# Weight loads of 512 KB through six buffers in place of 1 MB through three

## The chip, the cores and the metric

The kernel runs on one core of a Trainium2 chip. The metric is device time in microseconds (us) of one execution. The engines are TensorE (PE; PEld is its weight load), VectorE (DVE), ScalarE (ACT), GpSimd (POOL) and SyncE (SP). SP's queue issues the weight transfers.

## The reference

Two blocks of two layers each work on 256 rows of width 1024 in float32. A layer of the first block has a mixer (a linear recurrence, attention with a forget gate, retention), cross attention to a memory, and a gated feed-forward stage. A layer of the second block has a feed-forward stage, a second mixer (mixer2: sparse attention with compressed keys and values, two further attention branches, three gates), and another feed-forward stage. Cut to what loads weights:

```python
def swiglu(h, w_gate, w_up, w_down):
    return (jax.nn.silu(h @ w_gate) * (h @ w_up)) @ w_down
...
    def compress(t, w1, w2):
        blocks = t[:, cmp_idx] + cmp_pos[:, None, :]
        blocks = blocks.transpose(0, 3, 1, 2, 4).reshape(B, G, n_cmp, CMP_LEN * Dh)
        return jax.nn.silu(blocks @ w1) @ w2
```

## The kernel before

All weights are read once from HBM, some 366 MB, in the order in which they are used. Class `Weights` plans, loads and prepares them. `plan` cuts a matrix into *chunks*, one transfer each (two where halves or a second matrix are put side by side), and a chunk into *pieces*, the unit that products are made from. A chunk is up to `CHUNK` = 2048 numbers wide in each of 128 partitions, 1 MB; a piece up to `PIECE` = 1024, 512 KB. So most chunks hold two pieces.

`_load` takes the next chunk into one of `NRAW` = 3 buffers (tile `raw`) by a transfer on SP's queue. `_split` makes a piece usable: ScalarE casts it to a rounded high part (`whi`), VectorE subtracts that from the original for the low part (`wlo`). With the activations in two parts as well (`thi`, `tlo`), each product of float32 numbers is three products on TensorE: `whi,thi`, `wlo,thi`, `whi,tlo`. There are `NPIECE` = 6 buffers for split pieces, so `_split` runs up to five pieces ahead of the products.

When a chunk's last piece has been split, its `raw` buffer is released and `_load` is called for the next chunk at once. The weights of the compression in mixer2 (`nsa_cmp_k_w1_2`, `nsa_cmp_v_w1_2`) are planned with `split=False`: TensorE reads them from `raw`, and their buffer is released only in `done`, behind the products on the chunk's last piece:

```python
                if last:
                    self.made += 1
                    del self.raw[ci]
                    self._load()
                    continue
```

The order of all instructions is fixed when the program is built. `Pace` keeps an estimate of each engine's time, and `pump` puts side work (attention steps, norms) between the products when that estimate says it is ready. SP's queue is in order: a load that waits for its buffer holds back what stands behind it, the small transfers too (constants, memory rows, `kvd`, `hk`, `btiles`). Transfers of SP and ScalarE take eight semaphores in turn (DMAHW0 to DMAHW7), and each waits until the transfer that had its semaphore before, eight places earlier, has landed.

In mixer2, `plan_mixer2` puts the four compression chunks between the chunks of `w_in_2`, one behind each of the first chunks of columns 1816 and up. `nat_blocks` makes the products (accumulators `acc`), and a callback takes two compression pieces at the places `CMP_AT` (tiles `o<-raw`). Other names of the trace: `aux` and `o` are PSUM banks of the attention steps, `nngm` row maxima, `rn` and `rs` scores of two branches, `t` gate values and copies, `bt` bias tiles, `hk` bias rows read back from DRAM, `mem` the memory rows of the cross attention.

The program records through a helper, so that all its instructions have line 153; places are told by tile names.

Of the kernel before, what the change touches and what calls it, by code (L numbers as in the profile page):

```python
# [20 lines left out]
EPS = 1e-6  # L21
NEG = -1e30
NPIECE = 6
NRAW = 3
PIECE = 1024
CHUNK = 2048

CMP_AT = (1, 3, 5, 7)
RET_HEADS = 4
# [128 lines left out]
class Weights:  # L158


    def __init__(self, nc, ctx, tc):
        self.nc = nc
        self.raw_pool = ctx.enter_context(nc.pool(tc, name="w_raw", bufs=NRAW))
        self.pool = ctx.enter_context(nc.pool(tc, name="w_split", bufs=NPIECE))
# [4 lines left out]
    def plan(self, ap, c0, c1, k0, k1, a_chunk, a_piece, split=True, gain=None, halves=0, beside=None):  # L169

        b = c1 - c0
        if halves:
            v = ap.rearrange("(g r d) n -> g d r n", g=2, r=halves)
        for k in range(k0, k1, a_chunk):
            a = min(a_chunk, k1 - k)
            ci = len(self.chunks)
            if halves:
                parts = [(slice(64 * g, 64 * g + 64), v[g][:, k : k + a, c0:c1]) for g in (0, 1)]
            else:
                parts = [(slice(0, P), ap[k * P : (k + a) * P, c0:c1].rearrange("(a p) n -> p a n", p=P))]  # L180
            parts = [(ps, slice(0, b), v_) for ps, v_ in parts]
            if beside is not None:
                parts.append((slice(0, P), slice(b, 2 * b), beside[k * P : (k + a) * P, c0:c1].rearrange("(a p) n -> p a n", p=P)))
            self.chunks.append((parts, a, b * (1 if beside is None else 2)))
            for j in range(0, a, a_piece):
                n = min(a_piece, a - j)
                self.pieces.append([ci, j, n, b * (1 if beside is None else 2), split, j + n >= a, None, list(range(k + j, k + j + n)), gain])
# [7 lines left out]
    def _load(self):  # L195
        if self.loaded >= len(self.chunks):
            return
        parts, a, b = self.chunks[self.loaded]
        t = self.raw_pool.tile([P, CHUNK], F32, tag="raw", name=f"raw{self.loaded}")
        v = t[:, : a * b].rearrange("p (a n) -> p a n", a=a)  # L200
# [74 lines left out]
def tile_two_blocks(ctx, tc, I, out):  # L275
# [1680 lines left out]
    nc.sync.dma_start(x[:, 1, :], I["x"][0, P:, :])  # L1956
    for _ in range(NRAW - 1):
        W._load()
# [129 lines left out]
```

## Time and profile before

| | |
|---|---|
| median of 3 runs | 2094.27 us (2092.91 to 2097.39) |
| profiled execution | 2093.85 us, span of the core 2092.1 us |
| TensorE, busy | 2038.4 us, 97% of the span |
| VectorE, busy | 1251.7 us, 60% |
| ScalarE, busy | 1098.7 us, 53% |
| transfers | 380.79 MB, mean 182 GB/s |
| SP's queue | 366.46 MB, 52.9% of the 16 DMA engines' span |
| loads of `raw` from `w_in` | 65 of 1024 KB, median 5.2 us from issue to landing |

A row of a timeline gives start and duration in us, the engine, the operation, the tiles it writes and reads, the shape and a count; in brackets stands how long the engine had been idle and who ended that. In the chain of waits a row is a piece of the chain that ended last. Matmuls are pipelined, so their durations overlap.

### The profile page before, as it was taken

Reading aid. Unit: us, or ns where it says so; the run is one execution under the profiler, and the core shown is the slowest. Engines: PE = TensorE matmul, PEld = TensorE weight load, DVE = VectorE, ACT = ScalarE, POOL = GpSimd, SP = SyncE. Lnnn points to the kernel's source line nnn. Section 1 sums busy time; section 2 is a strip of 40 time slices with the busy share of each in tenths; the row PEclk is TensorE's granted clock in tenths of the full one; section 3 lists DMA queues with packets and bytes.
Section 4 is the critical chain, followed back from the end, with each engine's and each line's share of the span. In section 5 each row is a group of like instructions: output and inputs, shape, how many; then the busy total and the mean of one; then the engine's idle time right before and its main releaser. Section 6 shows DMA issues by size and latency. Waiting matters only on the chain.

```text
span 2092.1 us, 27297 instructions
## 1 busy us (share of the span) xinstructions
PE 2038.4 (97%) x10446; PEld 1675.9 (80%) x10446; DVE 1251.7 (60%) x2123; ACT 1098.7 (53%) x1844; POOL 89.6 (4%) x112
## 2 busy tenths in 40 slices
PE   7999999999999999999999999999999998999999
PEld 6788888888787788788887678888888886778887
DVE  6666565556764755555464667664555565666553
ACT  5556465445564654555445555553554455456542
POOL 0210000001200000000010000000000010000000
PEclk9999999999999999999999999999999999999999
DMA  7555565645465555555555455555555465455552
GB/s 241 184 189 194 184 202 181 219 153 195 162 222 171 184 199 191 165 197 181 204 173 194 137 147 181 192 175 196 181 187 193 163 192 197 132 155 188 176 199 102
DMA packets 200610, 380.79 MB, mean 182 GB/s; under 512 B 14288, under 2 KB 70400, under 8 KB 200480
## 3 DMA queue, kind: packets, MB, share of 16 engines
q1 hardware_dynamic: 188960, 366.46, 52.9%
q10 hardware_dynamic: 11520, 12.59, 1.9%
q8 instruction: 82, 1.34, 0.2%
q14 instruction: 48, 0.39, 0.1%
HBM read 372.03 MB, written 6.99 MB: 181 GB/s over the span
## 4 chain that ended last, share of the span: by engine, by line
PE 81%; DVE 6%; ACT 5%; DMA 4%; issue 2%; POOL 0%; SPq 0%; ACTq 0%; DVEq 0%; POOLq 0%
PE acc L153 73%; PE aux L153 6%; DVE wlo L153 2%; DMA raw<-in_w_in_dram 2%; PE o L153 2%; ACT whi L153 2%; DMA hk<-ud 1%; ACT rn L153 1%; DMA nb<-cdram 0%; ACT thi L153 0%; DVE h L153 0%; DMA bt<-btiles 0%; ACT cpr L153 0%; DMA mem<-in_mem_dram 0%; DVE tlo L153 0%
## 5 line engine op out<-in xcount | busy, mean ns | idle before, releaser
L153 PE MATMUL acc<-whi,thi 128*128 128x512 f32 (+1 forms) x1760 | 702.1, 399 | 4.5 <-ACT kvout L153 2.7
L153 PE MATMUL acc<-wlo,thi 128*128 128x512 f32 (+1 forms) x1760 | 683.0, 388 | 3.5 <-DVE wlo L153 3.3
L153 PE MATMUL acc<-whi,tlo 128*128 128x512 f32 (+1 forms) x1760 | 683.8, 389 | 2.4 <-DVE tlo L153 2.3
L153 DVE TENSOR_TENSOR wlo<-raw,whi 128x1024 fp32r<-128x1024 f32 (+1 forms) x370 | 444.7, 1213 | 313.8 <-ACT whi L153 311.6
L153 ACT CAST whi<-raw 128x1024 fp32r<-128x1024 f32 (+1 forms) x370 | 378.5, 1038 | 252.9 <-PE acc L153 195.5
L153 DVE SCALAR_TENSOR_TENSOR wlo<-raw,prm,whi 128x512 fp32r<-128x512 f32 (+1 forms) x592 | 392.6, 719 | 177.2 <-ACT whi L153 176.9
L153 ACT ACTIVATE whi<-raw,prm 128x512 fp32r<-128x512 f32 (+1 forms) x592 | 372.2, 696 | 92.9 <-PE acc L153 89.4
L153 PEld LDWEIGHTS acc<-whi,thi 128*128 128x128 f32 x1760 | 332.8, 189 | 80.1 <-issue 12.3
L153 PEld LDWEIGHTS acc<-whi,tlo 128*128 128x128 f32 x1760 | 332.2, 189 | 73.2 <-DVE tlo L153 5.5
L153 PEld LDWEIGHTS acc<-wlo,thi 128*128 128x128 f32 x1760 | 333.0, 189 | 67.5 <-DVE wlo L153 6.5
L153 PE MATMUL acc<-whi,ahi 128*128 128x512 f32 x528 | 206.8, 392 | 0.3
L153 PE MATMUL acc<-whi,alo 128*128 128x512 f32 x528 | 205.6, 389 | 0.0
L153 PE MATMUL acc<-wlo,ahi 128*128 128x512 f32 x528 | 205.5, 389 | 0.0
L153 POOL TENSOR_TENSOR r<-v,mhalf 128x1 f32<-128x1 f32 (+3 forms) x46 | 49.5, 1076 | 1661.0 <-DVE v L153 1661.0
L153 DVE SCALAR_TENSOR_TENSOR silu<-acc,r,silu 128x512 f32<-128x512 f32 (+1 forms) x72 | 47.5, 702 | 118.1 <-PE acc L153 94.1
L153 PEld LDWEIGHTS acc<-whi,ahi 128*128 128x128 f32 x528 | 99.1, 188 | 21.6 <-ACT whi L153 1.5
L153 PEld LDWEIGHTS acc<-whi,alo 128*128 128x128 f32 x528 | 99.1, 188 | 20.5
L153 PEld LDWEIGHTS acc<-wlo,ahi 128*128 128x128 f32 x528 | 99.2, 188 | 20.2
L153 PE MATMUL acc<-thi,whi 128*128 128x256 f32 x384 | 113.4, 295 | 0.0
L153 ACT ACTIVATE silu<-acc,r 128x512 f32<-128x512 f32 (+1 forms) x72 | 43.1, 650 | 127.5 <-PE acc L153 127.5
L153 PE MATMUL acc<-tlo,whi 128*128 128x256 f32 x384 | 108.5, 283 | 0.0
L153 PE MATMUL acc<-thi,wlo 128*128 128x256 f32 x384 | 108.5, 282 | 0.0
(299 smaller groups left out, 1823.9 us busy)
## 6 DMA issues: line engine op xcount, KB each, us to landing
raw<-in_w_in_dram SPq DMA_DIRECT2D x65, 1024.0 KB, 5.2
raw<-in_ffn_w_down_dram SPq DMA_DIRECT2D x44, 1024.0 KB, 4.8
raw<-in_ffn_w_gate_dram SPq DMA_DIRECT2D x40, 1024.0 KB, 5.0
raw<-in_ffn_w_up_dram SPq DMA_DIRECT2D x40, 1024.0 KB, 5.0
raw<-in_w_down_dram SPq DMA_DIRECT2D x22, 1024.0 KB, 4.9
raw<-in_w_gate_dram SPq DMA_DIRECT2D x20, 1024.0 KB, 5.0
raw<-in_w_up_dram SPq DMA_DIRECT2D x20, 1024.0 KB, 4.9
raw<-in_w_out_dram SPq DMA_DIRECT2D x16, 1024.0 KB, 4.9
```

Of the source, the lines that this page charges most:

```text
L153: return f(*args, **kwargs)
```

## The change

A chunk becomes 1024 numbers wide in each partition, and there are six buffers in place of three. `plan` reduces every chunk to the pieces that fit, at least one: a chunk of 512 columns is now two of the 128-row blocks of its matrix instead of four, one piece. The compression chunks are halved in the same way.

```diff
-NRAW = 3
+NRAW = 6
 PIECE = 1024
-CHUNK = 2048
+CHUNK = 1024
...
     def plan(self, ap, c0, c1, k0, k1, a_chunk, a_piece, split=True, gain=None, halves=0, beside=None):
 
         b = c1 - c0
+
+        a_chunk = min(a_chunk, max(1, CHUNK // (b * (1 if beside is None else 2)) // a_piece) * a_piece)
         if halves:
```

A load is now put in the program behind the release that stands six releases before it, where it was three chunks before. The start loads six chunks ahead instead of three.

SP's queue in the first mixer2, before (`raw175` and `raw177` are compression weights for keys, `raw179` for values; a DVE wait is for the subtraction behind which the load's buffer is free, a PE wait for products on compression weights):

```order
L153 DMA raw176_9415<-in_w_in_2_dram 128x4x512 [waits DMAHW4_49,DVE_49]
L153 DMA raw177_9470<-in_nsa_cmp_k_w1_2_dram 128x8x256 [waits DMAHW1_49,DVE_49]
L153 DMA raw178_9622<-in_w_in_2_dram 128x8x256 [waits DMAHW4_49,DMAHW2_49,DVE_49]
L153 DMA raw179_9670<-in_nsa_cmp_v_w1_2_dram 128x8x256 [waits DMAHW3_49,PE_49]
L153 DMA raw180_9704<-in_w_in_2_dram 128x4x512 [waits DMAHW2_49,DVE_49]
```

The same place in the changed program:

```order
L153 DMA raw350_9788<-in_nsa_cmp_k_w1_2_dram 128x4x256 [waits DMAHW4_49,DVE_49]
L153 DMA raw351_9824<-in_nsa_cmp_k_w1_2_dram 128x4x256 [waits DMAHW5_49,DVE_49]
L153 DMA raw352_9950<-in_w_in_2_dram 128x4x256 [waits DMAHW6_49,DVE_49]
L153 DMA raw353_9978<-in_w_in_2_dram 128x4x256 [waits DMAHW7_49,PE_49]
L153 DMA raw354_10022<-in_nsa_cmp_v_w1_2_dram 128x4x256 [waits DMAHW0_49,DVE_49]
L153 DMA raw355_10028<-in_nsa_cmp_v_w1_2_dram 128x4x256 [waits DMAHW1_49,PE_49]
L153 DMA raw356_10034<-in_w_in_2_dram 128x2x512 [waits DMAHW6_49,DMAHW2_49,DVE_49]
L153 DMA raw357_10064<-in_w_in_2_dram 128x2x512 [waits DMAHW7_49,DMAHW3_49,DVE_49]
```

`raw178` waited for the subtraction of `raw176`'s second piece; its first half, `raw352`, waits for that of the first piece, its second half, `raw353`, for the products on the first half of the first compression chunk. `raw180` waited for the subtraction of the second piece of `raw178`; its first half, `raw356`, waits for that of `raw352`.

A little later on the same queue, before:

```order
L153 DMA raw181_9742<-in_nsa_cmp_v_w1_2_dram 128x8x256 [waits DMAHW5_49,DMAHW1_49,PE_49]
L153 DMA raw182_9799<-in_w_in_2_dram 128x4x512 [waits DMAHW4_49,DMAHW0_49,DVE_49]
L153 DMA raw183_9859<-in_w_in_2_dram 128x4x512 [waits DMAHW3_49,PE_49]
L153 DMA raw184_9893<-in_w_in_2_dram 128x4x512 [waits DMAHW5_49,PE_49]
L153 DMA raw185_9919<-in_w_in_2_dram 128x4x512 [waits DMAHW0_49,DVE_49]
```

and in the changed program:

```order
L153 DMA raw360_10110<-in_w_in_2_dram 128x2x512 [waits DMAHW2_49,DMAHW0_49,DVE_49]
L153 DMA raw361_10163<-in_w_in_2_dram 128x2x512 [waits DMAHW3_49,DMAHW1_49,DVE_49]
L153 DMA raw362_10219<-in_w_in_2_dram 128x2x512 [waits PE_49]
L153 DMA raw363_10225<-in_w_in_2_dram 128x2x512 [waits PE_49]
L153 DMA raw364_10231<-in_w_in_2_dram 128x2x512 [waits DMAHW4_49,DMAHW0_49,DVE_49]
L153 DMA raw365_10261<-in_w_in_2_dram 128x2x512 [waits DMAHW5_49,DMAHW1_49,DVE_49]
```

`raw184` waited for the last products on the compression weights of `raw181` (PE); its first half, `raw364`, waits for the subtraction of `raw360`, the first half of the old `raw182`, and its second half for that of `raw361`.

At the start of the program, SP's queue before (`bd`, `bf`, `pos_i`, `freq` and `gain` are constants, `mem` the memory rows):

```order
L153 DMA raw6_178<-in_w_in_dram 128x4x512 [waits DMAHW1_49,DVE_49]
L153 DMA causal_22_196<-in_c128_dram 128x128 [waits DMAHW5_49]
L153 DMA ntri_23_198<-in_c128_dram 128x256
L153 DMA bd_24_200<-in_w_rg_dram 64x2x64 [waits Pool_49]
L153 DMA bd_24_200<-in_w_rg_dram 64x2x64 [waits DMAHW0_49]
L153 DMA bd_24_200<-in_w_ig_dram 64x2x64
L153 DMA bd_24_200<-in_w_ig_dram 64x2x64 [waits DMAHW2_49]
L153 DMA bf_25_206<-in_fox_b_f_dram 128x8 [waits DMAHW3_49]
L153 DMA pos_i_259<-in_positions_dram 128x2x1 [waits DMAHW4_49]
L153 DMA freq_38_262<-in_c128_dram 128x32 [waits DMAHW5_49]
L153 DMA gain_41_271<-in_mem_norm_g_dram 128x1024 [waits DMAHW6_49]
L153 DMA mem_42_273<-in_mem_dram 128x1024 [waits DMAHW7_49,PE_49]
```

and in the changed program:

```order
L153 DMA raw11_192<-in_w_in_dram 128x2x512 [waits DMAHW2_49,DVE_49]
L153 DMA causal_22_206<-in_c128_dram 128x128
L153 DMA ntri_23_208<-in_c128_dram 128x256 [waits DMAHW3_49]
L153 DMA bd_24_210<-in_w_rg_dram 64x2x64 [waits DMAHW4_49,Pool_49]
L153 DMA bd_24_210<-in_w_rg_dram 64x2x64 [waits DMAHW5_49]
L153 DMA bd_24_210<-in_w_ig_dram 64x2x64 [waits DMAHW6_49]
L153 DMA bd_24_210<-in_w_ig_dram 64x2x64 [waits DMAHW7_49]
L153 DMA bf_25_216<-in_fox_b_f_dram 128x8 [waits DMAHW0_49]
L153 DMA pos_i_269<-in_positions_dram 128x2x1 [waits DMAHW1_49]
L153 DMA freq_38_272<-in_c128_dram 128x32 [waits DMAHW2_49]
L153 DMA gain_41_281<-in_mem_norm_g_dram 128x1024 [waits DMAHW3_49]
L153 DMA mem_42_283<-in_mem_dram 128x1024 [waits DMAHW4_49,PE_49]
```

The constants keep their places behind the weights; `raw6` before and `raw11` now are the last weight loads ahead of them, and `pos_i` waits for the one that has landed on its semaphore, `raw6` (DMAHW4) before and `raw11` (DMAHW1) now. The weights queued ahead of `causal` are half a megabyte more.

On TensorE side work moves by a few products at seven places. In each mixer2 `o<-rn,vsw` stands three products later (27 products on a gate's weights ahead of it where 24 were, 6 behind it where 9 were), and a transposition (`aux<-ident,ta`) 15 small ones later.

## Rows read from the trace of the kernel before

**Rows 1.** The page, busy us of each engine (share of the span).

```profile
PE 2038.4 (97%) x10446; PEld 1675.9 (80%) x10446; DVE 1251.7 (60%) x2123; ACT 1098.7 (53%) x1844; POOL 89.6 (4%) x112
```

**Rows 2.** The chain of waits: start us, us, what; for a transfer the time to landing.

```profile
706.37 20.45 PE acc L153 x90
...
1109.93 5.30 DMA raw<-in_w_in_dram
...
1119.29 4.97 DMA raw<-in_w_in_dram
...
1142.00 5.82 DMA raw<-in_w_in_dram
```

**Rows 3.** The timeline of TensorE, products that ended a wait (columns as above).

```profile
43.49 0.66 PE L153 MATMUL aux<-ident,h 128*128 128x128 f32 x4 [0.68 <-DVE h L153]
...
648.88 1.10 PE L153 MATMUL aux<-hk,anti 128*128 128x512 f32 x2 [2.09 <-DMA hk<-ud]
...
1127.19 1.83 PE L153 MATMUL aux<-t 64*128 64x256 f32 x8 [2.58 <-DVE nngm L153]
...
1157.01 1.55 PE L153 MATMUL o<-rs,sv 128*64 128x256 f32 x8 [3.87 <-ACT t L153]
...
1735.41 2.20 PE L153 MATMUL aux<-t 64*128 64x256 f32 x8 [2.19 <-DVE nngm L153]
...
1765.88 1.02 PE L153 MATMUL o<-rs,sv 128*64 128x256 f32 x8 [3.10 <-ACT t L153]
```

**Rows 4.** Windows: stretch and length, busy us by engine, granted clock, DMA share, GB/s.

```profile
1127.20:1131.60 4.40, 4.40 (x20) 3.80 (x21) 2.43 (x9) 2.97 (x12) 0.00 (x0) 0.61 0.02 8
1157.00:1162.30 5.30, 5.29 (x21) 4.22 (x22) 3.97 (x10) 1.43 (x2) 0.00 (x0) 0.50 0.49 159
1735.40:1742.50 7.10, 7.09 (x34) 5.78 (x38) 3.09 (x10) 5.28 (x16) 0.00 (x0) 0.52 0.32 94
1765.90:1769.90 4.00, 4.00 (x18) 3.16 (x19) 3.85 (x10) 0.92 (x2) 0.00 (x0) 0.57 0.48 186
```

**Rows 5.** The timeline of VectorE, subtractions in the first mixer2.

```profile
1105.61 1.22 DVE L153 TENSOR_TENSOR wlo<-raw,whi 128x1024 fp32r<-128x1024 f32 x1 [1.98 <-ACT whi L153]
...
1108.68 1.22 DVE L153 TENSOR_TENSOR wlo<-raw,whi 128x1024 fp32r<-128x1024 f32 x1
...
1125.36 1.23 DVE L153 TENSOR_TENSOR wlo<-raw,whi 128x1024 fp32r<-128x1024 f32 x1 [5.17 <-ACT whi L153]
```

**Rows 6.** The timeline of ScalarE in the first mixer2.

```profile
1111.40 3.17 ACT L153 ACTIVATE rs<-rs 128x384 f32<-128x384 f32 x6
1115.25 1.05 ACT L153 CAST whi<-raw 128x1024 fp32r<-128x1024 f32 x1 [0.68 <-DMA raw<-in_w_in_dram]
...
1119.77 0.99 ACT L153 ACTIVATE rs<-rs 128x384 f32<-128x384 f32 x2 [0.72 <-DVE rs L153]
1124.28 1.05 ACT L153 CAST whi<-raw 128x1024 fp32r<-128x1024 f32 x1 [3.53 <-DMA raw<-in_w_in_dram]
...
1135.84 2.00 ACT L153 CAST whi<-raw 128x1024 fp32r<-128x1024 f32 x2 [1.29 <-DMA raw<-in_w_in_dram]
...
1141.08 0.86 ACT L153 COPY rn<-aux 128x384 f32<-128x384 f32 x2 [0.45 <-PE aux L153]
1147.84 1.05 ACT L153 CAST whi<-raw 128x1024 fp32r<-128x1024 f32 x1 [5.90 <-DMA raw<-in_w_in_dram]
```

**Rows 7.** The page's DMA issues: count, KB each, median us from issue to landing.

```profile
raw<-in_w_in_dram SPq DMA_DIRECT2D x65, 1024.0 KB, 5.2
...
raw<-in_ffn_w_gate_dram SPq DMA_DIRECT2D x8, 512.0 KB, 3.8
raw<-in_ffn_w_up_dram SPq DMA_DIRECT2D x8, 512.0 KB, 5.1
```

**Rows 8.** The timeline of SP's queue at the start.

```profile
26.40 0.38 SPq L153 DMA_DIRECT2D pos_i<-in_positions_dram  x1
...
27.88 0.37 SPq L153 DMA_DIRECT2D mem<-in_mem_dram  x1
```

## The prediction

> **What bounds the kernel now.** I read the page's busy shares first: TensorE is busy for 97% of the span [rows 1], so only time in which it stands still, or runs at its lower clock, can be won. In a weight stage it takes 90 products of 512 columns in 20.45 us [rows 2], 0.227 us each; a half of 512 KB feeds 12 of them and is used up in 2.73 us. Next, TensorE's timeline, for what ended its idle times. Once the first products run, the long ones lie in the two mixer2 blocks: 2.58 and 3.87 us in the first, 2.19 and 3.10 us in the second [rows 3], 11.74 us in all. The granted clock of the stretches that follow them comes from a table of windows [rows 4]: means of 0.61, 0.50, 0.52 and 0.57, where 1 is 2.4 GHz and 0.5 is 1.2 GHz. Then the ScalarE and VectorE timelines, to see whom TensorE waited for.
>
> The first stop, backwards: TensorE waits for row maxima (nngm) that VectorE makes just behind a weight subtraction (wlo at 1125.36, [rows 5]); that waits for ScalarE's cast (whi at 1124.28), and the cast waited 3.53 us for its weights [rows 6]. They were issued at 1119.29 and took 4.97 us [rows 2]. The second stop has the same root: the cast at 1147.84 waited 5.90 us [rows 6] for a load issued at 1142.00 [rows 2]; behind it ScalarE still has the exponentials, a table load and the copies that free the bank TensorE wants. So in these blocks the loads end last, although DMA is far from full: two of the three 1 MB buffers hold compression weights (nsa_cmp), which are not split and stay until their products are done, and one buffer is left for the stream.
>
> **The change part by part.** Every load becomes one piece. The bytes, the products and the casts stay, as do the 3 MB of buffers; SP's list grows from 443 rows to 794. In the steady weight stages a first half is now asked for one piece earlier, and nothing waits for it there: 0 us.
>
> *First stop.* raw178 went out at 1109.93 [rows 2], behind the subtraction of raw176's second half (1108.68 plus 1.22, [rows 5]). raw352, its first half, needs only the subtraction of the first half, over at 1105.61 + 1.22 = 1106.83. A 512 KB load takes 3.8 us by the nearest row and 5.2 us at most, the median of 1 MB [rows 7]; I take 3.8, since it has the same size. It lands at 1110.7, before ScalarE is free at 1111.40 + 3.17 = 1114.57 [rows 6], so the cast starts at 1114.6 in place of 1115.25. Its subtraction ends some 2.3 us later, at 1116.9, and raw356, the half that ended the stop, goes out then: 2.4 us sooner than the 1119.29 of raw180. It lands at 1120.7 (1122.1 by the upper bound); ScalarE is free at 1119.77 + 0.99 = 1120.76. The cast runs at 1120.8 in place of 1124.28, 3.5 us sooner (2.2 by the bound). The stop of 2.58 us goes, or 0.4 us of it stays. The second half, raw357, is asked for after the next subtraction and has the exponentials ahead of it: covered.
>
> *Second stop.* raw184 waited for the last product on the compression weights of raw181; raw364 waits for the subtraction of raw360 instead. ScalarE cast that half at 1135.84, after 1.29 us of waiting for a load [rows 6]; with the 3.5 us from above and without that wait it is at 1131.1, its subtraction ends 2.3 us later at 1133.4, and raw364 lands at 1137.2 (1138.6). ScalarE's copies before it, at 1141.08 for 0.86 us [rows 6], wait for TensorE, which is 2.58 + 1.72 us earlier (clock, below), so they end at 1137.6. The cast then runs at 1137.6 (1138.6) instead of 1147.84. To do away with the stop although TensorE itself comes 4.3 us sooner, it must run by 1147.84 - 3.87 - 4.3 = 1139.7: 1 to 2 us are to spare. Three products of 0.227 us move ahead of o<-rn,vsw just there, and six stay behind it, enough for the copy it feeds. Late next would be ScalarE's chain of exponentials, table load and copies.
>
> *Second block.* The same instructions, with shorter stops: both go, 2.19 + 3.10 us.
>
> *Clock.* Each of the four low stretches begins with a product that had just been waited for [rows 3, 4]; without the stops I see nothing ahead of them that would bring the clock down. What the low stretches cost is TensorE's busy time by the missing share of the clock [rows 4]: 4.40 x 0.39 + 5.29 x 0.50 + 7.09 x 0.48 + 4.00 x 0.43 = 1.72 + 2.65 + 3.40 + 1.72 = 9.49 us.
>
> *Small transfers.* A small one now stands behind 512 KB on SP's queue where 1 MB was. The wait of 2.09 us at 648.88 [rows 3], for hk, lies behind a gate load: between 0 and 2.09 us go; I take 1.0. Against that, at the start the memory rows are queued after pos_i, which waits for the last weight load to land (26.40, the mem load at 27.88, [rows 8]). That was raw6 and is now raw11, with half a megabyte more ahead. TensorE already waits 0.68 us for these rows at 43.49 [rows 3], so the delay is paid: 0 to 2.6 us, half of the 5.2 of 1 MB; I take 1.0, because raw11 can also go out earlier. VectorE's further semaphore waits, one per subtraction, fall into its 40% of idle time [rows 1]; in the stretches above they would take from the 1 to 2 us to spare.
>
> *Sum.* 11.74 + 9.49 + 1.0 - 1.0 = 21.2 us off the profiled execution's 2093.85 us (span 2092.1): 2072.6. That execution lies 0.42 us under the median of the runs, so 2073.0.
>
> The Trainium skill speaks against the change: "DMA: Bandwidth & Descriptors" (Anatomy of one DMA; Bandwidth) gives each transfer about 2.0 us that do not shrink with its size, and advises 1 MiB and more per transfer; paid one after another for the 351 added rows that would be 702 us and a time near 2796. The trace bears out the fixed part (3.8 us for half of what takes 5.2), not that it is paid one after another; what this would do here is the third rival.
>
> **The rivals.** (1) ScalarE takes the place of the load at the second stops. Its chain is in order and has 1 to 2 us to spare; if waits of a transfer for the one eight places before it, the semaphores or a 5.2 us landing use them up, TensorE stands there again and the clock falls again: 3.87 + 3.10 + 2.65 + 1.72 = 11.3 us come back, 2084.3. For it speaks that the margin is made of several links; against it, that each link is taken from a row. (2) Nothing moves: the half loads find their buffers no sooner, because the compression halves hold as many bytes as before, or the stops come back elsewhere in the block: 2092 to 2096, 2094. Against it: both decisive loads change the instruction they wait for, which the order shows; that the change does not do what it says is excluded by the same rows (each load is one piece long). (3) Slower: half loads follow each other too slowly. The point that decides is 2.73 us per half: if each must land before the next moves, a half takes 3.8 us, 1.07 us more than TensorE needs, and for the 130 halves of in_w_in's 65 loads alone that is 139 us, 2233. Against it: of the pair of 512 KB loads issued together in a feed-forward block, gate landed after 3.8 and up after 5.1 us [rows 7], so they overlap, and six may be under way.
>
> **How the numbers follow.** The forecast, 2073.0, has 0.66; rival 1 0.17, rival 2 0.10, rival 3 0.07. A measurement of this kernel tells about 0.2% (4.2 us) from no change. Faster by more than that are the forecast and rival 1, 0.83; within it rival 2, 0.10; slower 0.07. The range starts at 2067: the whole hk wait and no delay at the start (2.1 us), 0.68 us less at 43.49, the runs' own scatter of 1.4 us below the median, and 2 us for other small transfers that stand behind less. It ends at 2085, behind rival 1, and leaves out rivals 2 and 3 (0.17).
>
> **What would show it.** Right: no wait of 2 us or more on TensorE in the mixer2 blocks, a granted clock of 1.00 throughout them, and ScalarE's waits for in_w_in loads there near zero. In the first block the cast of the old raw180 3 to 4 us sooner against the cast before the exponentials at 1111.40; a landing of 3.8 us for 512 KB. Wrong: TensorE waits there for ScalarE's copies with the loads long landed (rival 1), or 512 KB take 5 us and more and land one by one, with casts waiting for loads in the feed-forward stages (rival 3). A longer wait than 0.68 us for h near 43.5 shows the price at the start; above 2.6 us I have underrated it.

## The result and the profile after

The changed kernel takes 2070.43 us (median of four runs, 2068.56 to 2072.21); the kernel before, beside it, 2095.83 us (2092.91 to 2099.35). The ratio is 0.9883, with a 95% interval of 0.9862 to 0.9904. The profiled executions, 2071.4 and 2093.85 us, stand 22.45 us apart. A second set of runs, told below, gave 2068.98 us and 0.9890.

The page first, against [rows 1]: TensorE is busy for 7.4 us less in a span that is 22.5 us shorter, so its share goes from 97 to 98%.

```profile
span 2069.6 us, 28365 instructions
PE 2031.0 (98%) x10446; PEld 1670.8 (81%) x10446; DVE 1250.3 (60%) x2123; ACT 1097.3 (53%) x1844; POOL 90.0 (4%) x112
```

TensorE's timeline, at the six places of [rows 3] (start us, us, operation; in brackets the wait ahead of it and what ended it):

```profile
44.56 0.99 PE L153 MATMUL aux<-ident,h 128*128 128x128 f32 x4 [1.95 <-DVE h L153]
...
650.08 1.10 PE L153 MATMUL aux<-hk,anti 128*128 128x512 f32 x2 [1.78 <-DMA hk<-ud]
...
1125.57 0.70 PE L153 MATMUL aux<-t 64*128 64x256 f32 x4
...
1149.37 0.87 PE L153 MATMUL o<-rs,sv 128*64 128x256 f32 x8
...
1722.28 1.00 PE L153 MATMUL aux<-t 64*128 64x256 f32 x8
...
1746.15 0.87 PE L153 MATMUL o<-rs,sv 128*64 128x256 f32 x8
```

The four products in mixer2 that had waited 2.58, 3.87, 2.19 and 3.10 us have no bracket left. The wait for `hk` is 0.3 us shorter; the one for `h` at the start is longer, 1.95 us in place of 0.68. The windows around these places (stretch and length, TensorE's busy us, granted clock, DMA share, GB/s) show the clock, against [rows 4]:

```profile
44.00:48.00 4.00, 3.44 (x17) 0.59 0.50 135
1120.00:1127.00 7.00, 7.00 (x66) 1.00 1.00 331
1143.00:1150.00 7.00, 7.00 (x40) 1.00 0.89 301
1719.00:1726.00 7.00, 7.00 (x61) 1.00 0.86 305
1742.00:1749.00 7.00, 7.00 (x44) 1.00 0.81 285
```

In mixer2 it is full throughout; behind the longer wait at the start it fell. ScalarE's timeline in the first mixer2, against [rows 6], shows the casts that had waited:

```profile
1115.51 1.03 ACT L153 CAST whi<-raw 128x1024 fp32r<-128x1024 f32 x1
1117.18 1.06 ACT L153 CAST whi<-raw 128x1024 fp32r<-128x1024 f32 x1
1121.32 1.04 ACT L153 CAST whi<-raw 128x1024 fp32r<-128x1024 f32 x1 [0.33 <-DMA raw<-in_w_in_dram]
...
1138.13 1.06 ACT L153 CAST whi<-raw 128x1024 fp32r<-128x1024 f32 x1
```

The wait of 3.53 us ahead of the third is 0.33, and the cast that waited 5.90 us at 1147.84 starts at 1138.13 without a wait. The loads behind them, on SP's queue:

```profile
1107.90 3.75 SPq L153 DMA_DIRECT2D raw<-in_w_in_dram  x2
1117.82 2.08 SPq L153 DMA_DIRECT2D raw<-in_w_in_dram  x2
```

`raw352` goes out at 1107.90, `raw356` at 1117.82, and 3.50 us later its cast runs; `raw180` needed 4.97 us from issue to landing [rows 2]. The page's list of DMA issues (count, KB each, median us to landing) has, for [rows 7]:

```profile
raw<-in_w_in_dram SPq DMA_DIRECT2D x132, 512.0 KB, 4.2
raw<-in_ffn_w_down_dram SPq DMA_DIRECT2D x88, 512.0 KB, 4.3
```

ScalarE's list of waits sums the casts' waits for these loads: 32.5 us in 16 waits before, now:

```profile
ACT whi L153 <- DMA raw<-in_w_in_dram: 6.8, 7, 4.2
```

To see where the time went, one product serves as a mark: the first transposition of `h` ahead of each mixer2, which waits 1.0 us in every version. TensorE's timeline of the kernel before, and of the changed one:

```profile
1062.86 0.63 PE L153 MATMUL aux<-ident,h 128*128 128x128 f32 x4 [1.01 <-DVE h L153]
...
1671.46 0.63 PE L153 MATMUL aux<-ident,h 128*128 128x128 f32 x4 [1.01 <-DVE h L153]
```

```profile
1063.99 0.63 PE L153 MATMUL aux<-ident,h 128*128 128x128 f32 x4 [1.02 <-DVE h L153]
...
1660.68 0.63 PE L153 MATMUL aux<-ident,h 128*128 128x128 f32 x4 [1.00 <-DVE h L153]
```

From mark to mark, the stretch with the first mixer2, it took 608.60 us and takes 596.69; from the second mark to the end of the span 420.64 and 408.92. So 11.91 and 11.72 us, together 23.6, come from the two stretches with a mixer2, and up to the first mark 1.1 us are lost in this execution (a second one, below, does not lose them).

### The profile page after: what moved, and what is told of

Read it like the earlier page. It is cut to its first block, busy times and chain, and to the rows that moved or that the text cites. A ratio compares the mean times of both kernels' runs of the same rounds, so it can differ in the third digit from the quotient of the medians.

```text
span 2069.6 us, 28365 instructions
## 1 busy us (share of the span) xinstructions
PE 2031.0 (98%) x10446; PEld 1670.8 (81%) x10446; DVE 1250.3 (60%) x2123; ACT 1097.3 (53%) x1844; POOL 90.0 (4%) x112
## 4 chain that ended last, share of the span: by engine, by line
PE 85%; DVE 6%; ACT 4%; DMA 2%; issue 2%; ACTq 0%; SPq 0%; POOL 0%; DVEq 0%; POOLq 0%
PE acc L153 76%; PE aux L153 7%; PE o L153 2%; DVE wlo L153 2%; ACT whi L153 1%; DMA kvd<-kvout 1%; ACT thi L153 0%; DMA raw<-in_w_in_dram 0%; ACT cpr L153 0%; DVE h L153 0%; DVE ngm L153 0%; DVE tlo L153 0%; DMA nb<-cdram 0%; DMA mem<-in_mem_dram 0%; DVE cv L153 0%
```

## Experiments

Two theories to start with. **A**, the prediction's: what a load has to wait for is over sooner, since half a buffer is given back at a time, so the load is issued sooner. **B**: the smaller transfer itself, which lands sooner after its issue. The times of TensorE's two stretches (mark to mark, and second mark to the end) tell the versions apart better than whole runs, since in versions without stops they agree within 1 us. Each is one execution; that of the kernel before stands in a scatter of 2085 to 2099 us, so the differences against it can be off by some us:

| version | first stretch | second | both, against before | run, us |
|---|---|---|---|---|
| kernel before | 608.60 | 420.64 | | 2093.85 (profiled) |
| changed kernel | 596.69 | 408.92 | -23.6 | 2070.43 |
| the same, second set | 596.61 | 408.40 | -24.2 | 2068.98 |
| half transfers, 1 MB buffers (and another buffer taken) | 598.80 | 412.25 | -18.2 | 2075.01 |
| 1 MB in mixer2 alone | 603.04 | 416.00 | -10.2 | 2082.68 |
| 1 MB outside mixer2 alone | 596.72 | 408.19 | -24.3 | 2071.71 |
| five halves | 599.17 | 411.65 | -18.4 | 2074.76 |
| 1 MB, another buffer taken | 603.84 | 415.76 | -9.6 | 2085.40 |
| half transfers, another buffer, sent early | 596.84 | 408.08 | -24.3 | 2068.70 |
| half transfers, another buffer, held | 599.45 | 411.60 | -18.2 | 2076.13 |
| four halves | 619.77 | 425.73 | +16.3 | 2114.87 |

### Half transfers into whole buffers

In the kernel before:

```diff
+        two = a * b > 1024 and len(parts) == 1
         for ps, cs, ap in parts:
-            self.nc.sync.dma_start(v[ps, :, cs], ap)
+            for js in ((slice(0, a // 2), slice(a // 2, a)) if two else (slice(0, a),)):
+                self.nc.sync.dma_start(v[ps, js, cs], ap[:, js, :])
```

> The kernel before with one edit: each 1 MB load is issued as two transfers of 512 KB into the same 1 MB buffer; three buffers, each still given back whole. Theory A (the gain comes from giving back half a buffer at a time, so that a load is issued sooner): the loads of the two stops go out when they did before, 1119.29 and 1142.00 in the first block; only their first halves land sooner, by 3.8 us after issue instead of 4.97 and 5.82, so each stop is shorter by 1 to 2 us (11.74 us of stops become about 5.5) and the clock still falls behind them: 2088 to 2092 against about 2095.8 for the kernel before. Theory B (the gain comes from the smaller transfer, which lands sooner): all four stops go, 2069 to 2074. Theory C (more transfers cost time, which the change made good elsewhere): slower than before, 2098 and more.

Measured: 2075.01 us (2074.64 to 2077.42), ratio 0.9932 (0.9918 to 0.9946); the kernel before took 2089.6 us beside it, with a spread from 2086.05 to 2094.61. The time lies far under theory A's range and just over theory B's: by the stretches three quarters of the gain are there, 18.2 of 23.6 us, although every buffer is still given back whole. SP's queue and ScalarE at the first stop:

```profile
1117.52 0.88 SPq L153 DMA_DIRECT2D raw<-in_w_in_dram  x2
```

```profile
1121.02 1.05 ACT L153 CAST whi<-raw 128x1024 fp32r<-128x1024 f32 x1 [2.04 <-DMA raw<-in_w_in_dram]
```

and TensorE's four stops:

```profile
1123.94 1.47 PE L153 MATMUL aux<-t 64*128 64x256 f32 x8 [0.30 <-DVE nngm L153]
...
1148.88 0.87 PE L153 MATMUL o<-rs,sv 128*64 128x256 f32 x8 [0.51 <-ACT t L153]
...
1722.82 1.47 PE L153 MATMUL aux<-t 64*128 64x256 f32 x8 [0.39 <-DVE nngm L153]
...
1747.77 0.87 PE L153 MATMUL o<-rs,sv 128*64 128x256 f32 x8 [0.51 <-ACT t L153]
```

The cast waits for the first half alone, 3.50 us behind its issue where the whole took 4.97: 1.47 us sooner. The cast before it had waited 0.68 us for the first half of the load ahead [rows 6] and no longer does, so the load itself goes out some 0.8 us sooner. Together that is the 2.28 us by which the first stop is shorter (2.58 to 0.30): theory B. I had expected the stops to be halved and the clock to stay low behind them; what is left of them did not bring it down.

The second stop is another matter. The expectation had its load, `raw184`, go out behind the last products on the compression weights of `raw181`, as before. In this program it does not: `raw184` and `raw185` have changed buffers (as has the same pair in the second mixer2), and `raw184` waits for the subtraction of `raw182`'s second half. The last products on `raw181` before, and then in this run; the chain of waits at this load; and on SP's queue the load behind it, `raw185`, which now waits for those products:

```profile
1141.30 0.64 PE L153 MATMUL o<-raw,t 128*32 128x256 f32 x8
```

```profile
1136.52 0.64 PE L153 MATMUL o<-raw,t 128*32 128x256 f32 x8
```

```profile
1136.17 3.51 DMA raw<-in_w_in_dram
```

```profile
1137.22 0.37 SPq L153 DMA_DIRECT2D raw<-in_w_in_dram  x1
```

The load goes out at 1136.17, ahead of the last eight products, 1.05 us before the one that waits for them; and its first half lands in 3.51 us where the whole took 5.82 [rows 2], 2.31 us less. Together that is the 3.36 us by which the stop is shorter (3.87 to 0.51). In the second mixer2 the two parts are 1.06 and 1.53 us, and the stop falls by 2.59. That TensorE comes to these products 4.8 us sooner takes nothing from the stop, since it comes to the stop that much sooner as well. So this run carries two edits, the smaller transfer and another buffer for a load in each mixer2. What the buffer is worth by itself is told below.

### 1 MB in one place, 512 KB in the other

Both versions hold the raw weights in one area of six half buffers, from which a 1 MB load takes two neighbouring halves; a flag per stage sets the size.

```diff
+        cap = 2 * CHUNK if self.wait else CHUNK
-        a_chunk = min(a_chunk, max(1, CHUNK // (b * (1 if beside is None else 2)) // a_piece) * a_piece)
+        a_chunk = min(a_chunk, max(1, cap // (b * (1 if beside is None else 2)) // a_piece) * a_piece)
...
+        if self.whole[self.loaded]:
+            got = next(([s & ~1, s | 1] for s in self.open if s ^ 1 in self.open), None)
+        else:
+            got = self.open[:1]
...
+            W.wait = True
             plan_mixer2(l)
+            W.wait = False
```

> The changed kernel, but in the two mixer2 blocks alone the weights are again loaded 1 MB at a time into pairs of neighbouring half buffers and given back whole; everywhere else 512 KB. Theory A with the place that the prediction named: all of the gain is in mixer2, so the four stops are back and the longer start stays: 2093 to 2097, no faster than the kernel before. Theory B or any that spreads the gain over the 351 added transfers (earlier landings in all stages): most of the gain stays, 2070 to 2082.

Measured: 2082.68 us, ratio 0.9963 (0.9951 to 0.9976). The first stops are there (2.15 and 2.09 us), the second ones are gone in the first mixer2 and 1.38 us long in the second, and 10.2 us of the gain stay. The expectation missed a second edit in this version: an area taken from this list is the one that the program gave back first, and so the load of the second stop waits for a subtraction and not for the products on compression weights. That became an experiment of its own, below.

> The mirror of the run before: 512 KB loads in the two mixer2 blocks alone, 1 MB loads into pairs of half buffers everywhere else. Theory A: the four stops stay away, and the start is that of the kernel before, so its wait for the memory rows is 0.68 us again and no clock is lost at 44.7: 2067 to 2071, 0 to 3 us faster than the changed kernel's 2070.4. Theory B (gain spread over all stages): 2082 to 2092.

Measured: 2071.71 us, ratio 0.9915 (0.9899 to 0.9930); stretches of 596.72 and 408.19 us, as in the changed kernel. The whole gain of the change is in mixer2: with 1 MB in all other stages nothing is lost. It was not faster than the changed kernel: its first mark comes at 1064.49, behind a wait of 2.78 us for `hk` with the clock at 0.50 from 648 to 652.

### Five buffers, and four

```diff
-NRAW = 6
+NRAW = 5
```

> The changed kernel with five buffers of 512 KB instead of six (2.5 MB). If the grain of giving back is all that matters, five do as well: 2069 to 2073. If the number of halves left for the stream beside the compression weights decides (four compression halves at most, so one is left instead of two), each load in mixer2 goes out one piece, 2.73 us, later, which is more than the 1 to 2 us that the prediction found to spare at the second stops: stops of 1 to 3 us come back there, with some of the lower clock behind them, 2075 to 2088.

> The changed kernel with four half buffers (2 MB) in place of six. Five cost a stop of 1.28 us in the first mixer2 block and 1.33 in the second, for one load issued a piece later. If each buffer less costs one piece (2.73 us) of issue time at those places, four give stops of 3 to 5 us at the first stops and some at the second ones, with the lower clock behind them: 2083 to 2100. If the smaller landing had made the number of buffers matter little: 2073 to 2078. In mixer1 and the feed-forward blocks four halves hold 10.9 us of TensorE's work against a landing of 3.5 to 4.5 us, so nothing is expected there.

Measured with five: 2074.76 us (2072.11 to 2076.64), ratio 0.9928 (0.9915 to 0.9942). The number of halves counts, as the second reading said, but the time lies just under its range, and the stops are not where it had them: 1.28 and 1.33 us at the first stops, none at the second ones, and the clock stays up.

```profile
1125.02 1.47 PE L153 MATMUL aux<-t 64*128 64x256 f32 x8 [1.28 <-DVE nngm L153]
...
1724.26 1.47 PE L153 MATMUL aux<-t 64*128 64x256 f32 x8 [1.33 <-DVE nngm L153]
```

With four: 2114.87 us, ratio 1.0107 (1.0089 to 1.0126), above my range. Stops of 3.52 and 2.96 us in the first mixer2, more behind it (2.46 and 2.69 us), and, against the expectation, 6 us lost ahead of the first mark (1069.00, before 1062.86). In the two stretches the sixth half buffer is worth 5.2 us, the fifth 34.7.

### The buffer that a load takes, alone

1 MB loads in 1 MB buffers, every compute engine's instructions as before; only the list of free areas of the version above decides where a load goes. In mixer2 that changes what three loads wait for, `raw184` to `raw186`, and the same three in the second one.

> The kernel before with 1 MB loads, 1 MB buffers given back whole and the same instructions in the same order on TensorE, VectorE, ScalarE and GpSimd; the one edit is that a load takes the buffer that the program gave back first, so that raw184 waits for the subtraction of raw182's second half and no longer for the last product on the compression weights of raw181. Theory A for the second stops (they come from the load that waits for compression weights): the first stops stay at 2 to 2.6 us with the clock down behind them, the second ones go or stay under 1.5 us: 2077 to 2083. Rival D (the second stop is only what the first one leaves behind, by its length and by the lower clock, so the buffer makes no difference): 2087 to 2093, as the kernel before.

Measured: 2085.40 us (2080.35 to 2088.52), ratio 0.9970 (0.9958 to 0.9982): between the two ranges. The mechanism is theory A's:

```profile
1128.11 2.20 PE L153 MATMUL aux<-t 64*128 64x256 f32 x8 [2.39 <-DVE nngm L153]
1155.95 0.87 PE L153 MATMUL o<-rs,sv 128*64 128x256 f32 x8 [0.84 <-ACT t L153]
...
1731.77 2.20 PE L153 MATMUL aux<-t 64*128 64x256 f32 x8 [2.17 <-DVE nngm L153]
1759.54 0.87 PE L153 MATMUL o<-rs,sv 128*64 128x256 f32 x8 [0.51 <-ACT t L153]
```

The first stops stay, the second ones fall from 3.87 and 3.10 us to 0.84 and 0.51, since `raw184` no longer waits for compression weights. The chain of waits at its load, and the products that it had waited for:

```profile
1141.69 5.08 DMA raw<-in_w_in_dram
```

```profile
1143.26 0.64 PE L153 MATMUL o<-raw,t 128*32 128x256 f32 x8
```

It goes out 2.2 us before they end. In the stretches the buffer is worth 9.6 us, near the 11.3 us at which the prediction priced the second stops with their clock; the ratio of the runs gives 6.3 us and their medians 7.7, with a wait of 3.04 us for `hk` ahead of the first mark in the profiled one. The runs scatter over 8 us.

### Half transfers, sent early and held

> The run before (1 MB buffers, given back whole, the buffer that was given back first is taken) with each 1 MB load issued as two transfers of 512 KB. If the shorter landing of the first half (3.5 us after issue in place of 4.9) is enough for the first stops and the buffer for the second ones, giving back half a buffer at a time is not needed at all: 2069 to 2073, the changed kernel's 2070.4 within its spread. If giving back halves is needed beyond that (theory A as the prediction had it): 2074 to 2080, with stops of over 1 us left in mixer2.

Measured: 2068.70 us (2067.61 to 2071.20), ratio 0.9895 (0.9876 to 0.9914), the changed kernel's time. But the version was not what its text says: SP's queue shows that its halves go out early.

```profile
1106.91 3.43 SPq L153 DMA_DIRECT2D raw<-in_w_in_dram  x2
```

That is 2.32 us behind the cast at 1104.59; in the changed kernel it is 2.32 us too, in the kernel before 5.39 (1109.93 behind 1104.54). A transfer into half of the area waits for that half alone, so this run repeats the change and tells nothing of holding. The next one holds, by laying the two halves the other way round every second time:

```diff
...
-            self.nc.sync.dma_start(v[ps, :, cs], ap)
+            for j in ((0, a // 2) if two else (0,)):
+                n, at = (a // 2, (j + turn) % a) if two else (a, 0)
+                self.nc.sync.dma_start(v[ps, at : at + n, cs], ap[:, j : j + n, :])
```

> The run with half transfers and the buffer that was given back first, once more, with the two halves of a load laid into their 1 MB buffer the other way round every second time. The trace of that run showed its first halves going out 2.32 us behind the cast at 1104.59, as in the changed kernel, not 5.4 us as in the one before: a transfer into half a buffer waits for that half alone. Laid the other way round, the first half goes where the later half was, so both go out only when the whole buffer is free; every engine's instructions and their order stay. From TensorE's timeline, the two mixer2 blocks took 596.84 and 408.08 us with early halves; 598.80 and 412.25 with half transfers alone, in buffers taken as before. If the size of the transfer and the buffer taken explain all: 596.5 to 597.3 and 408 to 409, 2068 to 2071. If sending halves early is needed too: 598 to 600 and 410 to 413 with stops of 0.3 to 1.5 us at the first stops, 2072 to 2076.

Measured: 2076.13 us (2075.02 to 2078.81), ratio 0.9920 (0.9903 to 0.9936). Its halves go out 5.38 us behind the cast at 1103.87, both at once:

```profile
1109.25 0.92 SPq L153 DMA_DIRECT2D raw<-in_w_in_dram  x2
...
1117.84 0.88 SPq L153 DMA_DIRECT2D raw<-in_w_in_dram  x2
```

```profile
1121.49 1.05 ACT L153 CAST whi<-raw 128x1024 fp32r<-128x1024 f32 x1 [2.19 <-DMA raw<-in_w_in_dram]
```

This pair has the same instructions in the same order and differs in the moment of issue alone: 24.3 us of gain with early halves, 18.2 with held ones. So sending a half as soon as its place is free is worth 6.1 us here, in waits of about half a microsecond at each of the four places and in later ones for `bc` and `wng` (1.22, 0.74 and 1.25 us; with early halves the last is 0.66 and the others are under 0.5).

The held version takes for `raw184` the buffer that the version with half transfers in 1 MB buffers takes, and stands at the same 18.2 us. It differs from the version with another buffer alone by the half transfers only. So the gain comes in three steps: 9.6 us by the other buffer for the loads of the second stops, 8.6 more by the half transfers, 6.1 more by sending halves early. The first and the third are theory A, a load that is issued sooner because what it waits for is over sooner; the second is theory B. As each step is read from single executions, they are good to a few us.

The order of the steps matters. Half transfers with `raw184` still behind the products on `raw181` were not run. By the rows of the first experiment its load would go out 1.05 us later and leave a stop of some 1.6 us (an estimate, 0.51 + 1.05) where the buffer alone leaves 0.84; so a part of the 9.6 us could be had by either, and how much of the 18.2 us the transfers would bring by themselves stays open.

### Transfers of 256 KB

In the changed kernel, 492 loads more on SP's queue (1286 for 794):

```diff
-            self.nc.sync.dma_start(v[ps, :, cs], ap)
+            for js in ((slice(0, a // 2), slice(a // 2, a)) if a > 1 and a * b > 512 else (slice(0, a),)):
+                self.nc.sync.dma_start(v[ps, js, cs], ap[:, js, :])
```

> The changed kernel with each 512 KB load issued as two transfers of 256 KB into the same half buffer, over 600 transfers more. If transfers overlap and only their landing counts: 2069 to 2073. If each transfer has a price of its own on the queue (the third rival of the prediction), a half is two of them: the loads fall behind the 2.73 us in which TensorE uses up a half, 2100 and more. In between, if the eight semaphores limit what is under way (eight times 256 KB in place of six times 512 KB): stops of about 1 us in mixer2, 2073 to 2080.

Measured: 2069.70 us (2068.22 to 2070.95), ratio 0.9897 (0.9878 to 0.9915): no price for twice as many transfers, and no gain. The page's DMA issues:

```profile
raw<-in_w_in_dram SPq DMA_DIRECT2D x264, 256.0 KB, 3.6
```

A quarter of the bytes of the old load lands in 3.6 us where the whole took 5.2 and the half 4.2. By these three medians some 3 us of a landing do not shrink with the bytes (an estimate), yet they are not paid one after another, since the loads overlap.

### The start

> The changed kernel with the positions and the first memory rows queued behind raw7 instead of behind raw11. If the longer wait at the start (1.95 us for h near 44.6, and 3.4 us at half the clock behind it, 1.7 us) is the price of the weights that stand ahead of them, both go: 2066 to 2068 against the changed kernel's 2070.4. If the wait has another root (VectorE's own chain): 2070 to 2071.

Measured: 2081.55 us, ratio 0.9955 (0.9940 to 0.9970), 11 us slower than the changed kernel. The wait for `h` was gone and the clock at 1.00 from 40 to 60; but the planner had put TensorE's work in another order behind it, and waits of 4.35 and 5.19 us came at 106.80 and 138.69. As a test of the start's price it says nothing. The next two runs were made for that.

> The changed kernel once more, beside the next two, to see which of its profile's lines stay. No stop of 1.3 us or more in mixer2: certain by either theory. At the start: if the 1.95 us for h near 44.6 and the lower clock behind it belong to the change, both are there again; if they are the scatter of one execution (the variants with 512 KB transfers showed at most 0.5 us there), the wait is 0 to 0.7 us and the clock stays at 1.00. 2068 to 2072 either way.

Measured: 2068.98 us (2068.61 to 2070.74), ratio 0.9890 (0.9874 to 0.9906). The wait is 0.24 us, the clock full:

```profile
42.92 0.66 PE L153 MATMUL aux<-ident,h 128*128 128x128 f32 x4 [0.24 <-DVE h L153]
```

The first mark stands at 1061.89, 1 us before that of the kernel before. The 1.95 us of the first profile were the scatter of one execution.

```diff
...
+    early["src"] = gpool.tile([P, D], F32, tag="h", name=nm("mem"))
+    tc.nc.sync.dma_start(early["src"], I["mem"][0, :P, :])
     W._make_upto(NPIECE)
```

> The changed kernel with one DMA moved: the first memory rows are queued behind raw7 instead of behind raw11, the positions and everything else stay where they are, and no other engine's instructions move (unlike the run with the positions and the memory norm ahead, where the planner moved TensorE's work too and waits of 4.35 and 5.19 us came at 106.8 and 138.7). If the start price is real: 1 to 3.6 us faster than the changed kernel beside it. If it is scatter: within 1 us of it.

Measured: 2066.07 us (2064.33 to 2067.49), ratio 0.9873 (0.9854 to 0.9893), 2.9 us under the changed kernel beside it, and no run of the one reaches a run of the other. It is the fastest version of the study. TensorE's wait for `h` near 43 is gone, and the first mark comes at 1059.00, although its first product started 1.3 us later (10.52 for 9.23).

## Why the prediction was right, and where its reasons were not

**The number.** 2073.0 was forecast and 2070.43 measured, inside the range of 2067 to 2085; the gain was 21.2 us by the sum and 22.45 between the profiled executions.

**The four stops and the clock** went as the sum had them: 11.74 and 9.49 us, all in mixer2, and TensorE is busy for 7.4 us less although 1.7 us of low clock came up at the start; there was nothing elsewhere (the version with 1 MB in all other stages shows it). The stretches gave 23.6 us for 21.2; the rest is in smaller waits that I had not counted, such as TensorE's 1.14 us for `bc` behind the first mixer2 (0.39 now) and 1.26 us for `wng` in the second (none now).

**The first stop, link by link.** `raw356` was to go out at 1116.9, land 3.8 us later and be cast at 1120.8. With the mark 1.1 us later, that is 1118.0 and 1121.9; the trace has 1117.82, 3.50 us and 1121.32. `raw364`'s cast was to run at 1137.6 and ran at 1138.13, without a wait. So the first rival, ScalarE in the load's place, had its chance in the margin and did not come. The bound of 5.2 us "at most" for 512 KB held at these loads but was none: the list of [rows 7] has another row of 512 KB loads in the kernel before, with a median of 6.9 us.

```profile
raw<-in_w_up_nsa_dram SPq DMA_DIRECT2D x8, 512.0 KB, 6.9
```

**The weight of the causes.** The sum booked 2.4 us of the first stop to the earlier issue and 1.2 us to the shorter landing, and the second stop to the instruction that the load waits for; the second rival was set aside because "both decisive loads change the instruction they wait for". For the second stops the runs bear this out: with 1 MB transfers and that instruction alone changed they fall from 3.87 and 3.10 us to 0.84 and 0.51. For the first stops they do not: with 512 KB transfers and both halves held until the whole buffer is free, these fall from 2.58 and 2.19 us to 0.46 and 0.58. The landing, booked with 1.2 us, does nearly all of it by itself, 1.47 us at the load and some 0.8 at the load ahead of it. The earlier issue is there too, 2.6 us (1117.82, less the 1.1 us of the mark, for 1119.29), but the first stop all but goes without it. The sum asked for 3.5 us where 2.58 were enough, and a sum over links does not show that one of its links nearly does alone. So the causes were all real, and the total came out right though one weight in it was off. What issuing early would bring with transfers of 1 MB was not tried, since a half can't be sent early in one transfer with the other.

**What the total owes to one execution.** The 9.49 us of clock were read from one profiled execution of the kernel before, whose mean granted clock was 0.995. In another set its runs go from 2085.45 us at 0.999 to 2096.51 at 0.994, and 0.005 of the span is 10.5 us. So the clock term is not paid in full by every run, and that gain and sum agree within 1.3 us is in part luck.

**The start and hk.** +1.0 and -1.0 were booked. The first profile seemed to show the former (1.1 us at the mark, 1.95 us of wait), the second execution has -1.0 at the mark and 0.24 us of wait. Both terms are below what one profile can tell; the rows behind the first were right in that memory rows further ahead on the queue are worth 2.9 us, but not in that the change makes them later by a price that shows.

**The third rival.** 256 KB transfers, 492 of them more, cost nothing. (The change itself added 349 rows to SP's queue, 794 for 445 in the traces; the prediction counted 443, and so 351.) The rule of the Trainium skill ("DMA: Bandwidth & Descriptors", Bandwidth) that advises transfers of 1 MiB and more, measured there on transfers issued from GpSimd, does not decide for this stream. The landing has a fixed part, as that page says (Anatomy of one DMA): it took 3.6, 4.2 and 5.2 us for 256, 512 and 1024 KB. But while several are under way only the one that is waited for counts, and for that one 512 KB were better than 1 MB, and 256 KB no better than 512.

## What to carry to other kernels

Where an engine waits for a load, take the wait apart: what the load itself waits for before it goes out, and how long it then takes to land. Here both paid. Two loads, one in each mixer2, waited for a buffer that held weights which stay long while another was free sooner; taking the other was worth 9.6 us without one more transfer. Cutting the transfer to what the first cast needs gave 8.6 us more, and sending each half as soon as its place was free another 6.1. Before a gain is put down to the size of a transfer, look at what the decisive loads waited for: cutting them can change which buffer they take, as it did in the first experiment. And run the same kernel's profile twice before a wait of a microsecond or two is put down to the change.

## What the runs showed of the hardware that I had not expected

The length of a wait does not settle by itself whether the granted clock falls behind it. Waits of 1.28 and 1.33 us (five halves) left it at 1.00; those of 2.09 to 3.87 us at the four stops, in the versions with 1 MB transfers, were followed by some 3.4 to 7 us at 0.5. But the changed kernel's wait of 1.95 us at 44.56 was followed by 3.4 us at 0.5, while the wait of 2.09 us for `hk` in the kernel before [rows 3] left it at 1.00; in two other versions that same wait was 2.78 and 3.04 us long, and there the clock fell. The window behind the second of them:

```profile
648.00:652.00 4.00, 3.39 (x9) 0.73 0.49 185
```

Nor does it settle it at one and the same product. Behind the wait for `bc` in the second mixer2 the clock fell after 1.23 us (half transfers, 1 MB buffers) and stayed up after 1.25 us (half transfers, held):

```profile
1788.70:1792.70 4.00, 3.97 (x15) 0.71 0.48 143
```

```profile
1789.90:1793.90 4.00, 4.00 (x20) 1.00 0.47 134
```

The runs of the kernel before scatter over 11 us in one set and those of the version with another buffer over 8, those of the other versions by 2 to 5 us. In the kernel before the slow runs are those with the lower mean clock (above): a part of the time that the change won was also the part that varied.
